# Strassen's seven products for a split-float32 w_up, with token blocks of 264, in a one-core decoder trunk

## The chip, the cores and the metric

The kernel runs on one core of one Trainium2 chip. The metric is device time in microseconds (us) of one execution. A profiled execution gives a page and a trace with its own span. The engines are named as the profile names them: PE (matmul), PEld (its weight loads), DVE (VectorE), ACT (ScalarE), POOL (GpSimd), SP (SyncE, whose queue issues the DMAs).

## The reference, cut to what matters

One layer runs over 1024 prompt tokens and 8 sample sequences of 4 tokens, 1056 tokens in all. The model width is 1024; the FFN is 2 x 2816 wide. Everything is float32.

```
mixed = (sigmoid(m_a) * br_a + sigmoid(m_b) * (gl_1 * sigmoid(gl_2))) @ w_out   # gl = gelu(ys) @ w_s5_glu
x  = layer_norm(DN_ALPHA * x + g1 * mixed, ln1_g, ln1_b)
u2 = x * (1 + sc2) + sh2                    # sc2, sh2 per sequence
hf = u2 @ w_ffn_up                          # 1024 -> 2 x 2816
f  = (silu(hf[..., :2816]) * hf[..., 2816:]) @ w_ffn_down
x  = layer_norm(DN_ALPHA * x + g2 * f, ln2_g, ln2_b)
```

What comes before (w_in, an RG-LRU branch, an S5 state-space branch, w_lru_out) is the same in both kernels.

## The kernel before, in words

**Products.** Features lie on the 128 partitions, tokens along the free axis. A float32 number x is kept as hi (x rounded to float32r, which PE multiplies at the faster rate) and lo (x - hi, again float32r). A product is hi·hi + hi·lo + lo·hi: three matmuls for each k tile of 128 features, all summed in one PSUM bank (`mm`, L328). The tokens go in three blocks of 352 (`NB`), so one output tile of 128 features by 1056 tokens over 8 k tiles is 3 x 8 x 3 = 72 matmuls of 352 columns.

**Weights.** `WTile` holds one weight tile. Its load (L207, on SP's queue) brings the raw float32 tile; `split` makes the hi part by an ACT copy (L216) and the lo part by a subtraction (`lo_part`, which ends in the helper `tt`, L108), in two halves, of 512 columns when the tile has 8 k tiles. The subtraction runs on POOL (`self.e = P`), and on DVE for some tiles of w_out and of the last w_down part. The list `seq` fixes the order of the tiles; loads run up to three ahead of use, and the next tile is split while the current one is multiplied.

**Helpers.** All DVE and POOL tensor-tensor operations stand at L108 (`tt`), the scalar-tensor-tensor ones at L117 (`stt`). In the changed kernel the same helpers stand at L113 and L122.

**Order of work.** `tick()` stands ahead of each token block of a product; `later(n, fn)` hands a piece of work to the n-th tick from now. Beyond that each engine runs its instructions in the order in which the program writes them.

**Stages.** GLU: 16 tiles of w_glu, each by the three token blocks; the gate arithmetic is done by DVE, and the mixed activations are split by ACT and POOL into region `r2` (from L1129). w_out: all eight tiles stay in SBUF and the blocks of tokens go through them one after another (`by_tokens`). The residual x goes into M by DVE (L117, `m_t<-ps,small_t,m_t`). `Norm` centers M by the mean of its first tile (`center`, POOL), squares it (ACT L1217), sums it over the tiles (`add`, `add2`, DVE), and sums over the partitions with a small float32 matmul (L1228; the shift is L1205); `inv` takes the reciprocal (L1244). `norm1` subtracts the mean, multiplies by the inverse root, scales (ACT) and splits (ACT L1284, POOL) for the FFN.

**FFN.** The 22 k tiles of the hidden width go in four chunks (5, 5, 6, 6): for each hidden tile j two w_up tiles, gate and value, 72 matmuls each; then eight w_down tiles over the chunk's k tiles. Per token block the gate's evacuation is a tanh by ACT (L1344) and one DVE `stt`; the value's evacuation is a DVE product (L108, `norm_t<-norm_t,ps`), an ACT copy for hi (L1352) and a POOL subtraction for lo (`f_t<-norm_t,f_t`). The FFN's hidden activations of a chunk stay in SBUF (region `f`) until its w_down products. The last w_down part goes by blocks of tokens again, with the second norm (`norm2`) and the stores of y between.

## Time and profile before

| what | us |
| --- | --- |
| time, median of 3 runs | 1875.53 (1873.6 to 1875.69) |
| span of the profiled execution | 1876.2 |
| PE busy | 1766.6 (94%) |
| DVE busy | 974.8 (52%) |
| POOL busy | 798.3 (43%) |
| ACT busy | 619.9 (33%) |

For the profiled execution no time beside its span is given. The busy shares are averages over stages; the windows by stage and the chain of waits tell which engine sets the end. A matmul's record ends with the pipeline, so its duration in the rows (326 ns in the mean) is longer than the distance from one start to the next; that distance is what counts in a row of matmuls. The page writes the PE matmuls of a product under the line of `mm`, L328.

In the tables below "before" rows are instruction groups of the old kernel and "after" rows those of the new one; x3 means three in a row.

### The profile page before, as it was taken

The page shows a single profiled execution, that of the slowest core. Times are in us where ns is not written, and L with a number is a line of the kernel's source. Part 1 is how long each engine was busy: PE and PEld are TensorE (multiplying, and loading weights), DVE is VectorE, ACT ScalarE, POOL GpSimd, SP SyncE. Part 2 cuts the span into 40 slices and gives each one's busy share as a digit, 9 for nine tenths or more (in the row PEclk, how much of TensorE's full clock was granted, in tenths as well). Part 3 has the DMA queues.
Part 4 walks back from the last instruction along what each step waited for, and adds up shares of the span by engine and source line. Part 5 has one row for each costly group of instructions (what it writes and reads, how often), then busy time and mean ns, then how long its engine had stood idle before and what let it go on. Part 6 is the DMA issues. An engine that isn't in the chain of part 4 may idle for free.

```text
span 1876.2 us, 28961 instructions
## 1 busy us (share of the span) xinstructions
PE 1766.6 (94%) x11640; PEld 1724.6 (92%) x11640; DVE 974.8 (52%) x1560; ACT 619.9 (33%) x1212; POOL 798.3 (43%) x663
## 2 busy tenths in 40 slices
PE   6899989899898899999999799999999999999994
PEld 5899988899788899999999799999999999999984
DVE  6989999648888743333248841231132112211297
ACT  4433333345554633212224552112211221122233
POOL 3557666427666622233342543223323332233435
PEclk9999999999899899999999999999999999999997
DMA  9334544431111158533351010111111111111111
GB/s 342 108 106 135 161 146 140 130 123 60 48 41 59 48 139 246 172 123 126 137 198 65 23 45 26 43 58 49 35 51 57 46 37 43 57 46 43 51 35 67
DMA packets 89846, 171.92 MB, mean 92 GB/s; under 512 B 18928, under 2 KB 54000, under 8 KB 89712
## 3 DMA queue, kind: packets, MB, share of 16 engines
q1 hardware_dynamic: 89712, 170.07, 28.1%
q8 instruction: 91, 1.49, 0.3%
q14 instruction: 43, 0.35, 0.1%
HBM read 136.86 MB, written 29.02 MB: 88 GB/s over the span
## 4 chain that ended last, share of the span: by engine, by line
PE 60%; DVE 19%; POOL 8%; issue 8%; ACT 3%; DMA 2%; SPq 0%; POOLq 0%; ACTq 0%; DVEq 0%
PE ps L328 57%; DVE s_t L108 8%; DVE norm_t L108 2%; POOL weights_t L108 2%; POOL lru_t L108 2%; DVE m_t L108 2%; POOL r_t L108 2%; DVE left_t L108 2%; DVE s_t L760 1%; DVE m_t L117 1%; PE ps L387 1%; DVE s_t L117 1%; POOL m_t L108 1%; DVE small_r_t L472 1%; DVE small_l_t L472 0%
## 5 line engine op out<-in xcount | busy, mean ns | idle before, releaser
L328 PE MATMUL ps<-r_t,weights_t 128*128 128x352 f32 x7632 | 1262.3, 326 | 2.2 <-ACT weights_t L216 1.1
L328 PEld LDWEIGHTS ps<-r_t,weights_t 128*128 128x128 f32 x7632 | 1236.7, 191 | 15.5 <-issue 8.9
L108 POOL TENSOR_TENSOR weights_t<-small_t,weights_t 128x512 fp32r<-128x512 f32 (+2 forms) x260 | 344.0, 1341 | 598.3 <-ACT weights_t L216 542.0
L216 ACT ACTIVATE weights_t<-small_t 128x512 fp32r<-128x512 f32 (+2 forms) x262 | 145.7, 599 | 257.1 <-PE ps L328 137.1
L328 PE MATMUL ps<-f_t,weights_t 128*128 128x352 f32 x1206 | 194.5, 322 | 0.0
L328 PEld LDWEIGHTS ps<-f_t,weights_t 128*128 128x128 f32 x1206 | 193.7, 188 | 0.0
L117 DVE SCALAR_TENSOR_TENSOR norm_t<-norm_t,ps 128x352 f32<-128x352 f32 x66 | 34.4, 521 | 222.4 <-ACT norm_t L1344 222.4
L108 DVE TENSOR_TENSOR s_t<-s_t 128x128 f32<-128x128 f32 (+3 forms) x200 | 134.4, 719 | 12.7 <-ACT s_t L737 7.0
L108 DVE TENSOR_TENSOR norm_t<-norm_t,ps 128x352 f32<-128x352 f32 x66 | 34.4, 521 | 195.8 <-PE ps L328 195.6
L117 DVE SCALAR_TENSOR_TENSOR m_t<-ps,small_t,m_t 128x352 f32<-128x352 f32 (+1 forms) x120 | 68.4, 570 | 126.9 <-PE ps L328 126.8
L108 POOL TENSOR_TENSOR f_t<-norm_t,f_t 128x352 fp32r<-128x352 f32 x66 | 62.7, 951 | 154.0 <-ACT f_t L1352 154.0
L117 DVE SCALAR_TENSOR_TENSOR glu_t<-glu_t,ps 128x352 f32<-128x352 f32 x48 | 24.2, 518 | 185.3 <-PE ps L328 126.3
L328 PE MATMUL ps<-r_t,f_t 128*128 128x352 f32 x648 | 107.1, 326 | 0.1
L328 PEld LDWEIGHTS ps<-r_t,f_t 128*128 128x128 f32 x648 | 105.0, 190 | 1.6 <-issue 0.5
L1352 ACT ACTIVATE f_t<-norm_t 128x352 fp32r<-128x352 f32 x66 | 32.8, 498 | 200.9 <-DVE norm_t L108 200.9
L117 DVE SCALAR_TENSOR_TENSOR lru_t<-lru_t 128x1056 f32<-128x1056 f32 (+1 forms) x52 | 81.9, 1574 | 30.6 <-ACT lru_t L998 16.6
L108 POOL TENSOR_TENSOR m_t<-m_t,norm_t 128x352 f32<-128x352 f32 x58 | 62.4, 1101 | 76.7 <-ACT norm_t L1206 64.8
L117 DVE SCALAR_TENSOR_TENSOR lru_t<-lru_t,small_t 128x352 f32<-128x352 f32 (+2 forms) x96 | 87.9, 916 | 3.4
L1344 ACT ACTIVATE norm_t<-ps 128x352 f32<-128x352 f32 x66 | 30.6, 464 | 177.1 <-PE ps L328 177.1
L108 POOL TENSOR_TENSOR left_t<-s_t 128x512 f32<-128x512 f32 (+1 forms) x40 | 77.0, 1947 | 5.8 <-DVE s_t L108 3.5
L328 PE MATMUL ps<-f_t,r_t 128*128 128x352 f32 x378 | 63.7, 327 | 0.9 <-POOL r_t L108 0.5
L328 PEld LDWEIGHTS ps<-f_t,r_t 128*128 128x128 f32 x378 | 61.0, 188 | 2.7 <-POOL r_t L108 0.8
(210 smaller groups left out, 1586.4 us busy)
## 6 DMA issues: line engine op xcount, KB each, us to landing
small_t<-in_w_up_dram SPq DMA_DIRECT2D x44, 512.0 KB
small_t<-in_w_in_dram SPq DMA_DIRECT2D x40, 512.0 KB
small_t<-in_w_ada_dram SPq DMA_DIRECT2D x32, 512.0 KB
ada_w_t<-in_w_ada_dram SPq DMA_DIRECT2D x16, 512.0 KB
small_t<-in_w_glu_dram SPq DMA_DIRECT2D x16, 512.0 KB
small_t<-in_w_down_dram SPq DMA_DIRECT2D x16, 384.0 KB
small_t<-in_w_down_dram SPq DMA_DIRECT2D x16, 320.0 KB
d_u<-left_t SPq DMA_DIRECT2D x64, 72.0 KB
```

Source lines behind the costliest of these rows:

```text
L108: e.tensor_tensor(out, a, b, op=op)
L117: e.scalar_tensor_tensor(out, a, s, b, op0=op0, op1=op1)
L216: A.activation(self.hi[:, s], self.raw[:, s], AF.Copy)
L328: PE.matmul(out[:, :NB], a[:, k, :], x[:, h, nb, k, :], start=bool(first and n == 0 and q == 0), stop=bool(last and n == len(kts) - 1 and ...
L387: PE.matmul(b[32 * j:32 * j + 32, :128], silu_c[:, 2 * i + k, :], w.raw[:, k, 128 * j:128 * j + 128], start=i == k == 0, stop=i == 3 and k ...
L472: getattr(V, name)(*a, **k)
L760: V.tensor_tensor_scan(wf[:, 512 * r:512 * r + 512], tv[:, :512], vv[:, r].rearrange("p n c -> p (n c)"), 0.0, op0=OP.mult, op1=OP.add)
L1344: A.activation(p, b[:, :NB], AF.Tanh, scale=0.5)
L1352: A.activation(frr[:, 0, nb, k, :], p, AF.Copy)
```

## The change: what it does

From the GLU on the tokens go in four blocks of 264 (`Q`), by a new `mmq`. PSUM gives six rotating banks there; two more hold the sums of a norm.

w_out runs in two passes, token blocks 0 and 2 first (p = 0), 1 and 3 then (p = 1), so its tiles are loaded and split twice. The four token blocks pair up: blocks s and s + 2 form the two token halves of "s". After each pass, `norm_jobs` makes the mean and inverse root for its pair, and `operand_steps` the seven operands that Strassen's products (in Winograd's form) need: sums and differences of the two feature halves and the two token halves, each split into hi and lo. The residual of s = 0 is stored to DRAM (`d_x`) and read back later.

w_up: for hidden tile j the 2 x 2 block matrix has gate and value as its outputs and the two halves of the 1024 features as its inputs. `prep` makes seven weight operands of 4 k tiles (512 columns) from the two raw tiles: four DVE additions, seven ACT copies (hi), seven subtractions (lo: on POOL, or on DVE for most in the first units). Seven products of 4 x 3 = 12 matmuls take the place of eight, for each j and each s. `UNITS` orders them: hidden tiles 0 to 2 for s = 0, the same for s = 1, and from tile 3 on both s together, product by product. `prep` runs three products ahead (`LEAD`), with a ring of five places. `up_evac` adds the products up and makes the gate on two token blocks at once (264 x 2 = 528 columns): the last product v = 6 of an s is followed by a DVE addition, a POOL product, an ACT copy, a POOL subtraction, and a DMA that stores the finished hidden tile to DRAM (`d_f`).

w_down reads the hidden tiles back from DRAM (`f_load`, 1.08 MB each) into the places of the operands that are done with: 14 of them during the last unit and the rest later, on the same SP queue as the w_down tiles. It goes in five parts, `DOWN`, and the last part by token blocks with the second norm.

The matmuls that change are 6480 of 352 columns (GLU 1152, w_out 576, w_up 3168, w_down 1584) into 8112 of 264 (GLU 1536, w_out 768, w_up 22 x 2 x 7 x 12 = 3696, w_down 2112). The other 3456 stay.

```diff
-CHUNKS = (5, 5, 6, 6)
+DOWN = ((0, 4), (4, 8), (8, 13), (13, 16), (16, 22))
+Q = 264
+UNITS = [(j, (0,)) for j in range(3)] + [(j, (1,)) for j in range(3)] + [(j, (0, 1)) for j in range(3, FFT)]
...
-            self.e = V if key[0] == "out" and key[1] > 1 or key[0] == "down" and key[1] in DOWN_V else P
+            self.e = P
...
+    for p in range(2):
         for m in range(8):
-            queue("down", io["w_down"][m][:, k0:k0 + kc], (k0, m), nk=kc)
-        k0 += kc
-
-    # w_out, and w_down's last part, stay whole: they go through the blocks of tokens
+            queue("out", io["w_out"][m], (p, m))
+    for k0, k1 in DOWN:
+        for m in range(8):
+            queue("down", io["w_down"][m][:, k0:k1], (k0, m), nk=k1 - k0)
...
+    def mmq(out, w, x, kts, first=True, last=True, check=False):
+        kts = list(kts)
+        for n, k in enumerate(kts):
+            for q, (a, h) in enumerate(((w.hi, 0), (w.hi, 1), (w.lo, 0))):
+                PE.matmul(out[:, :Q], a[:, k, :], x(h, k), start=bool(first and n == 0 and q == 0),
+                          stop=bool(last and n == len(kts) - 1 and q == 2), skip_group_check=check)
+    def glu_product(w, evac):
+        for q in range(4):
+            tick()
+            b = bank()
+            mmq(b, w, lambda h, k: r1w[:, h, k, Q * q:Q * q + Q], range(8))
+            evac(q, b)
...
+    banks[0] = 6
...
+    def normal(ln, s, c):
+        for q in (s, s + 2):
+            x = halves(M[:, q])[:, :, 2 * c:2 * c + 2]
+            for h in range(2):
+                tt(V, x[:, h], x[:, h], over(ln.b[q][0][:, None, :Q], 2, Q), OP.subtract)
+            for h in range(2):
+                tt(V, x[:, h], x[:, h], over(ln.r[q][:, None, :], 2, Q), OP.mult)
...
+    def to_operand(e, v, s, c, x):
+        o, f = operand(v, s), operand(v, s, FT)
+        A.activation(o[:, 0, 2 * c:2 * c + 2], x, AF.Copy)
+        lo_part(e, o[:, 1, 2 * c:2 * c + 2], x, f[:, 0, 2 * c:2 * c + 2])
...
+        b11, b12, b21, b22 = t
+        return (
+            lambda: (modulated(s, 0, c, b11), modulated(s + 2, 0, c, b12)),
+            lambda: (to_operand(P, 1, s, c, b11), modulated(s + 2, 1, c, b22)),
+            lambda: (tt(V, b11, b12, b11, OP.subtract), to_operand(V, 2, s, c, b11)),
+            lambda: (tt(V, b12, b22, b12, OP.subtract), to_operand(P, 3, s, c, b12)),
+            lambda: (tt(V, b11, b22, b11, OP.subtract), to_operand(V, 0, s, c, b11), modulated(s, 1, c, b21)),
+            lambda: (to_operand(P, 5, s, c, b22), to_operand(V, 4, s, c, b21)),
+            lambda: (tt(V, b21, b21, b11, OP.subtract), to_operand(P, 6, s, c, b21)),
...
+    ring = [(wb, 1024 - z), (wb, 3072 - z), (xa, 56 * Q), (wb, z), (wb, z + 2048)]
...
+    LEAD = 3
...
+        g, p = raw4[2 * u % 4], raw4[(2 * u + 1) % 4]
+        a11, a12, a21, a22 = g[:, :4], g[:, 4:], p[:, :4], p[:, 4:]
+        if v == 0:
+            tt(V, s1t, a21, a22, OP.add)
+            tt(V, s2t, s1t, a11, OP.subtract)
+        if v == 3:
+            tt(V, a21, a11, a21, OP.subtract)
+        if v == 5:
+            tt(V, s2t, a12, s2t, OP.subtract)
+        src = (s2t, a11, s1t, a21, a12, s2t, a22)[v]
+        rg, o = ring[i % 5]
+        w = parts[i] = Part()
+        w.hi, w.lo = rg.v(o, 4, 128, t=FR), rg.v(o + 512, 4, 128, t=FR)
+        A.activation(w.hi, src, AF.Copy)
+        lo_part(V if len(UNITS[u][1]) == 1 and v % 3 != 2 else P, w.lo, src, rg.v(o, 4, 128))
+        if v == 6:
+            later(1, unit_load, u + 2)
...
+    for p in range(2):
+        for m in range(8):
+            w = use_w("out", (p, m))
+            for q in (p, p + 2):
                 tick()
+                mmq(b, w, lambda h, k: mixr[:, q, h, k, :], range(8))
+                block(ln, q, m, b, 16)
...
+        a, b, c = (bk[i][:, :Q] if i in bk else None for i in "abc")
+        cc, u2, ff = ev[bk["set"]]
+        c21, c22, f1, f2 = cc[:, 0], cc[:, 1], ff[:, 0], ff[:, 1]
+        if v == 1:
+            A.activation(c21, a, AF.Copy)
+            tt(V, u2, b, c21, OP.add)
+        elif v == 3:
+            tt(V, c22, b, c21, OP.add)
+            tt(V, c22, c, c22, OP.add)
+        elif v == 4:
+            A.activation(f1, a, AF.Tanh, scale=0.5)
+            stt(V, f1, f1, 1.0, a, OP.add, OP.mult)
+        elif v == 5:
+            tt(V, u2, c, u2, OP.add)
+            A.activation(f2, u2, AF.Tanh, scale=0.5)
+            stt(V, f2, f2, 1.0, u2, OP.add, OP.mult)
+        elif v == 6:
+            tt(V, c21, b, c21, OP.add)
+            tt(P, ff, ff, cc, OP.mult)
+            A.activation(fb[:, 0, :, s], ff, AF.Copy)
+            lo_part(P, fb[:, 1, :, s], ff, fbf[:, 0, :, s])
+            SP.dma_start(d_f[j].rearrange("p h (a s t) -> p h a s t", a=2, s=2)[:, :, :, s], fbf[:, :, :, s])
...
+    order = [(i, v) for v in range(7) for i in range(2)]
+    slots = order[:8] + order[8:13] + [order[13], (1, 7), order[0]] + order[1:7]
...
+    def f_load(k):
+        SP.dma_start(f_tile(k, FT), d_f[k])
...
+    for u, (j, ss) in enumerate(UNITS):
+        bk = {s: {"set": s if len(ss) > 1 else u % 2} for s in ss}
+        for v in range(7):
+            for s in ss:
+                tick()
+                k = "bacbacb"[v]
+                if v < 3:
+                    bk[s][k] = bank()
+                w, x = parts[7 * u + v], operand(v, s)
+                mmq(bk[s][k], w, lambda h, k: x[:, h, k, :], range(4), first=v < 3, check=True)
+                up_evac(j, v, s, bk[s])
+                if u == n - 1:
+                    f_load(slots.index((s, v)))
+            prep(7 * u + v + LEAD)
+            if u == n - 1 and v == 0:
+                residual_in(2)
+                cap[0] = first_down + 1
+                pump()
+            if u == n - 1 and v == 3:
+                cap[0] = len(seq)
+                pump()
+                split_to(first_down + 1)
...
+    for c, (k0, k1) in enumerate(DOWN[:-1]):
+        for m in range(8):
+            w = use_w("down", (k0, m))
+            for q in (0, 1, 3, 2):
+                tick()
+                b = bank()
+                mmd(b, w, q, k0, k1)
+                residual(b, 40, q, m)
+        for k in ((15, 16, 17, 18), (19, 20, 21), (), ())[c]:
+            f_load(k)
...
+    ws = [next_w("down", (LASTK, m)) for m in range(8)]
+    for q in ORDQ:
+        for m in range(8):
+            tick()
+            if q == ORDQ[0]:
+                split_to(seq.index(ws[min(m + 2, 7)]) + 1)
+            b = bank()
+            mmd(b, ws[m], q, LASTK, FFT)
+            block(ln, q, m, b, 40, q == 0 and m == 7)
+        if q:
+            later(2, ln.sums, q)
+            later(2, inv2, q)
+            for k in range(8):
+                later(3 + 2 * k // 3, norm2, q, k, P if k % 3 == 0 else V)
```

Three places of the programs, engine by engine.

POOL inside the FFN before (weights_t is the lo part of a w_up tile's half, f_t<-norm_t,f_t the lo part of a hidden tile's block of tokens):

```order
L108 TENSOR_TENSOR f_t<-norm_t,f_t 128x352 x3
L108 TENSOR_TENSOR weights_t<-small_t,weights_t 128x512 x4
L108 TENSOR_TENSOR f_t<-norm_t,f_t 128x352 x3
L108 TENSOR_TENSOR weights_t<-small_t,weights_t 128x512 x2
L108 TENSOR_TENSOR weights_t<-small_t,weights_t 128x256
```

POOL across the border between two double units after (weights_t and xa_t<-… 128x512 are lo parts of weight operands; small_t<-small_t and resid_t<-resid_t,small_t 128x528 are the products of gate and value for s = 0 and s = 1, r_t their lo parts):

```order
L113 TENSOR_TENSOR weights_t<-small_t,weights_t 128x512
L113 TENSOR_TENSOR small_t<-small_t 128x528
L113 TENSOR_TENSOR r_t<-small_t,r_t 128x2x264
L113 TENSOR_TENSOR resid_t<-resid_t,small_t 128x528
L113 TENSOR_TENSOR r_t<-resid_t,r_t 128x2x264
L113 TENSOR_TENSOR xa_t<-resid_t,xa_t 128x512
```

The product of gate and value moved from DVE to POOL; at the border four POOL instructions on hidden tiles stand between the lo part of the next unit's second weight operand (first row) and that of its third (last row).

DVE in one tick of w_out's second block of tokens before, with the first norm of the block ahead beside it:

```order
L117 SCALAR_TENSOR_TENSOR m_t<-ps,small_t,m_t 128x352
L108 TENSOR_TENSOR norm_t<-norm_t,m_t 128x352
L108 TENSOR_TENSOR m_t<-m_t,norm_t 128x352
L108 TENSOR_TENSOR m_t<-m_t,small_t 128x352
L108 TENSOR_TENSOR norm_t<-m_t,small_t 128x32
L108 TENSOR_TENSOR norm_t<-norm_t,small_t 128x32
L108 TENSOR_TENSOR norm_t<-norm_t 128x352
```

DVE in the first Strassen unit after (resid_t and small_t 128x528 are the first norm of s = 1 on two tiles of 264; 128x512 with weights_t or resid_t are weight operands; r_t and xa_t are activation or weight operands; what reads ps evacuates products or takes a norm's mean):

```order
L113 TENSOR_TENSOR resid_t<-small_t,resid_t 128x512
L113 TENSOR_TENSOR resid_t<-resid_t,ps 128x528 x2
L113 TENSOR_TENSOR resid_t<-resid_t 128x528 x2
L113 TENSOR_TENSOR resid_t<-resid_t,ps 128x528 x2
L113 TENSOR_TENSOR resid_t<-resid_t 128x528 x2
L113 TENSOR_TENSOR small_t<-ps,small_t 128x264 x2
L113 TENSOR_TENSOR weights_t<-small_t,weights_t 128x512
L113 TENSOR_TENSOR resid_t<-resid_t,small_t 128x32 x4
L122 SCALAR_TENSOR_TENSOR small_t<-small_t,ps 128x264
L113 TENSOR_TENSOR resid_t<-resid_t 128x512
L113 TENSOR_TENSOR resid_t<-resid_t,small_t 128x512
L113 TENSOR_TENSOR xa_t<-resid_t,xa_t 128x512
```

The norm of s = 1, the weight operands and the operand differences now stand in one DVE row with the evacuations of the first products.

SP's queue around the last w_down part before:

```order
L207 DMA small_t<-in_w_down_dram 128x640 x8
L207 DMA small_t<-in_w_up_dram 128x1024 x12
L207 DMA small_t<-in_w_down_dram 128x768 x8
L207 DMA small_t<-in_w_up_dram 128x1024 x12
L207 DMA small_t<-in_w_down_dram 128x768 x8
```

SP's queue during the last Strassen unit after (xa_t and r_t<-d_f are the hidden tiles that come back):

```order
L1499 DMA xa_t<-d_f 128x2112
L1499 DMA r_t<-d_f 128x2112
L1485 DMA resid_t<-d_x 128x2112
L216 DMA small_t<-in_w_down_dram 128x512
L1499 DMA xa_t<-d_f 128x2112
L1499 DMA r_t<-d_f 128x2112
L1499 DMA xa_t<-d_f 128x2112
L1499 DMA r_t<-d_f 128x2112
L1499 DMA xa_t<-d_f 128x2112
L1499 DMA r_t<-d_f 128x2112
L216 DMA small_t<-in_w_down_dram 128x512 x3
```

The loads of hidden tiles stand ahead of the second, third and fourth w_down tile in the queue.

## The prediction

> **What bounds the kernel now.** I read the page's busy shares first, then windows by stage (w_out with the first norm from 950, the norm's middle from 1041, the FFN from 1082, its last part from 1770), then the chain of waits.

> ```profile
> PE 1766.6 (94%) x11640; PEld 1724.6 (92%) x11640; DVE 974.8 (52%) x1560; ACT 619.9 (33%) x1212; POOL 798.3 (43%) x663
> core 0: us, PE busy (x) PEld busy (x) DVE busy (x) ACT busy (x) POOL busy (x), PEclk, DMA share, GB/s
> 950.00:1082.00 132.00, 120.40 (x757) 116.48 (x756) 103.75 (x180) 61.86 (x118) 60.10 (x55) 0.97 0.25 89
> 1041.00:1080.00 39.00, 30.85 (x194) 30.46 (x192) 33.59 (x42) 23.51 (x47) 25.80 (x23) 0.93 0.08 28
> 1082.00:1770.00 688.00, 688.00 (x4278) 687.75 (x4277) 144.79 (x273) 147.22 (x295) 221.13 (x208) 1.00 0.14 45
> 1082.73 686.91 PE ps L328 x4272
> ```

> In the FFN PE is never idle: DVE works 21% of it, POOL 32%. There only the number of matmuls and the price of one count. The chain's one step gives that price: 686.91 / 4272 = 160.8 ns for a matmul of 352 columns. In the w_out window PE lacks 132.00 - 120.40 = 11.6 us, and DVE, at 103.75, is the engine closest behind.

> **The columns.** 6480 matmuls of 352 become 8112 of 264. No product of 264 float32r columns is in the trace; small float32 ones are, of 136 columns (two start together, 0.23 us from the next two: 115 ns each) and of 352 (the first record of a pair ends 0.292 us before the second: 0.75 - 0.458).

> ```profile
> 176.56 0.39 PE L797 MATMUL ps<-left_t,s_t 128*128 128x136 f32 x2
> 176.79 0.39 PE L798 MATMUL ps<-s_t,left_t 128*128 128x136 f32 x2
> 1040.59 0.75 PE L1205 MATMUL ps<-m_t,small_t 128*128 128x352 f32 x2
> L1205 PE MATMUL ps<-m_t,small_t 128*128 128x352 f32 x12 | 4.5, 458 | 0.0
> ```

> These two give 0.82 ns for a column and some 4 ns fixed. With half that for a float32r column the 160.8 leave 16.5 ns fixed, and 264 columns cost 125 ns. Bounds: 120.6 in proportion to columns; 142 on the straight line from 115 at 136 to 160.8 at 352. I take 125, since the float32 pair shows a price nearly proportional to columns. Before: 6480 x 0.1608 = 1042.0 us; now 8112 x 0.125 = 1014.0: **-28** (-64 to +110). By stage: GLU +7, w_out +3, w_up -47, w_down +9. So the seventh part saved on w_up is all there is to win, and the other stages pay for the shorter block.

> [...]

> **The border between double units.** Nineteen units do two s at once: 168 matmuls, 21.0 us at 125 ns, against 144 x 0.1608 = 23.2 us for the two tiles before. What can hold PE is a weight operand whose lo part POOL has not made.

> ```profile
> L108 POOL TENSOR_TENSOR weights_t<-small_t,weights_t 128x512 fp32r<-128x512 f32 x130 | 167.9, 1312 | 331.4 <-ACT weights_t L216 287.4 <-DMA small_t<-in_w_ada_dram 43.6 <-POOL r_t L108 0.2
> L108 POOL TENSOR_TENSOR f_t<-norm_t,f_t 128x352 fp32r<-128x352 f32 x66 | 62.7, 951 | 154.0 <-ACT f_t L1352 154.0
> L216 ACT ACTIVATE weights_t<-small_t 128x512 fp32r<-128x512 f32 x130 | 74.7, 622 | 132.9 <-DMA small_t<-in_w_glu_dram 45.3 <-DMA small_t<-in_w_lru_out_dram 42.9 <-PE ps L328 27.3
> L1344 ACT ACTIVATE norm_t<-ps 128x352 f32<-128x352 f32 x66 | 30.6, 464 | 177.1 <-PE ps L328 177.1
> L108 DVE TENSOR_TENSOR norm_t<-norm_t,ps 128x352 f32<-128x352 f32 x66 | 34.4, 521 | 195.8 <-PE ps L328 195.6
> ```

> Count from the end of product 5 of the second s. DVE adds (0.43, scaled from 0.521), ACT makes the tanh (0.40) and then, behind it in its own order, the hi of the next unit's second operand (0.62); POOL makes its lo (1.31): 2.76. Product 6 of the first s ended at 1.5, so POOL goes on with its gate product of 528 columns (1.35, from 951 at 352 and 1312 at 512), waits for the ACT copy (0.64), makes the lo (1.35); the same for the second s; and only then comes the lo of the third operand (1.31). Together 2.76 + 6.68 + 1.31 = 10.75, and 0.3, an estimate, for the hand-overs: 11.05. PE has six products before it needs that operand: 72 x 0.125 = 9.0. It waits 2.05 us, at 18 borders: **+37**. Below: nothing, if POOL is a quarter quicker. Above +59, if each of its eight operations here takes 0.15 longer, as the 1.47 of the row further down against 1.31. Throughput is no trouble: POOL has 7 x 1.31 + 4 x 1.35 = 14.6 us of work in 21. A double unit then lasts 23.05 us, and in the steady part Strassen saves a tenth of a us on a pair of tiles.

> **The second w_out pass and units 0 to 2.** PE has 384 + 3 x 84 matmuls here, 79.5 us. DVE has 210 instructions by its order: 93 of 512 or 528 columns, 81 of 232 or 264, 4 reciprocals, 32 of 32 columns.

> ```profile
> L108 DVE TENSOR_TENSOR weights_t<-small_t,weights_t 128x512 fp32r<-128x512 f32 x2 | 1.3, 682 | 0.0
> L108 DVE TENSOR_TENSOR s_t<-left_t 128x256 f32<-128x256 f32 x6 | 2.3, 419 | 0.0
> L1244 DVE RECIPROCAL small_t<-norm_t 128x352 f32<-128x352 f32 x6 | 14.1, 2354 | 0.2
> L108 DVE TENSOR_TENSOR norm_t<-m_t,small_t 128x32 f32<-128x32 f32 x8 | 1.5, 192 | 0.7
> ```

> 93 x 0.68 + 81 x 0.43 + 4 x 1.77 + 32 x 0.19 = 111 us. The next rows are of the window from 1041; the last two, of the timeline, show that a DVE operation beside a POOL one takes 1.27 where it takes 0.52 alone.

> ```profile
> L108 DVE TENSOR_TENSOR m_t<-m_t,norm_t 128x352 f32<-128x352 f32 x8 | 7.5, 934 | 0.0
> L108 DVE TENSOR_TENSOR norm_t<-norm_t,m_t 128x352 f32<-128x352 f32 x7 | 6.7, 952 | 1.3 <-POOL m_t L108 1.1
> L108 DVE TENSOR_TENSOR m_t<-m_t,small_t 128x352 f32<-128x352 f32 x8 | 6.5, 809 | 0.3
> L108 DVE TENSOR_TENSOR norm_t<-norm_t 128x352 f32<-128x352 f32 x7 | 5.8, 825 | 2.9 <-ACT norm_t L1217 2.9
> L108 DVE TENSOR_TENSOR norm_t<-norm_t,small_t 128x352 f32<-128x352 f32 x1 | 1.2, 1230 | 0.1
> L108 POOL TENSOR_TENSOR weights_t<-small_t,weights_t 128x512 fp32r<-128x512 f32 x4 | 5.8, 1469 | 0.3 <-POOL r_t L108 0.2
> 1060.59 1.27 DVE L108 TENSOR_TENSOR m_t<-m_t,norm_t 128x352 f32<-128x352 f32 x1
> 1061.90 0.52 DVE L108 TENSOR_TENSOR m_t<-m_t,small_t 128x352 f32<-128x352 f32 x1
> ```

> 31 operations take 27.7 us, and would take 31 x 0.521 = 16.2 alone: 11.5 us for the window's 23 POOL operations, 0.50 us each. The stretch has 61 (41 in the pass, 20 in the units): 31 us. DVE needs 142 us, PE waits 142 - 79.5 = 62.5, of which 11.6 was waited before: **+51**. Bounds: +20 without collisions; +66 at 0.75 for each POOL operation, +82 with the waits for ACT and POOL that the window shows (4.5 in 39 us, so 16 in 142). The first pass (DVE about 22 us beside 48 of PE) and units 3 to 5 (33 beside 31.5) I put at nothing; PE covers them, and without that cover they cost the 2 us.

> **Hidden tiles through DRAM.** Each stored tile is 1.08 MB; the page's first slice shows what the queues move when nothing else counts, 342 GB/s.

> ```profile
> GB/s 342 108 106 135 161 146 140 130 123 60 48 41 59 48 139 246 172 123 126 137 198 65 23 45 26 43 58 49 35 51 57 46 37 43 57 46 43 51 35 67
> ```

> That is 3.16 us a tile. On SP's queue nine such transfers stand ahead of the second w_down tile: 28 us, begun 1.5 us into the last unit of 23 and issued only as its products end, so that tile lands some 10 us after the unit. It is due 6 us after (48 matmuls), with its split some 5 us late; six more tiles stand ahead of the fifth, which may be late by as much. The stores of the units before, 1.08 MB in 23 us, lie beside products. **+10** (0 to +25).

> **The last w_down part.**

> ```profile
> 1769.47 3.04 PE L328 MATMUL ps<-f_t,weights_t 128*128 128x352 f32 x18
> 1830.32 17.71 PE L328 MATMUL ps<-f_t,r_t 128*128 128x352 f32 x108
> L108 POOL TENSOR_TENSOR weights_t<-small_t,weights_t 128x384 fp32r<-128x384 f32 x34 | 34.4, 1015 | 63.0 <-ACT weights_t L216 55.1 <-PE ps L328 8.0
> ```

> Before, it took 1848.03 - 1769.47 = 78.6 us for 432 matmuls, 69.5 of work: 9.1 waited. Now a block of 264 is 18 us of PE. DVE has 22 operations in its sums and residual (9.5), the inverse (3.5) and five of eight tiles of the norm (4.3), and 13 POOL collisions (6.5): 23.8, three times 5.8 too much; in the first block POOL has 8 lo parts in two pieces (16 x 1.015) and 7 centers (7 x 0.75): 21.5, 3.5 too much. 17.4 + 3.5 - 9.1 = **+12** (-5 without collisions, +20 if the split falls late too). After the last matmul 1876.2 - 1848.0 = 28.2 us are left, more than half of it vector work on 352 columns, now 264: **-4**.

> Sum: 1876.2 - 28 + 37 + 51 + 10 + 12 - 4 = **1954**. The profiled execution stands 0.7 us above the median of the runs, 1875.53, and I leave that out.

> **Rivals.**
> *POOL is quick enough.* [...] If an operation of 528 columns took 1.0 us (the chain then is 11.05 - 6 x 0.34 = 9.0: from there the border costs nothing) and DVE lost nothing beside it, the sum is -28 + 0 + 20 + 10 - 5 - 4 = -7: **1869**, 1859 with the transfers hidden. For it speaks that POOL is idle two thirds of the FFN; against it, that 1312 is a mean of 130 operations beside a nearly idle DVE. 0.19.
> *Everything collides.* Stretch +82, border +59, transfers +25, last part +20, less 32: **2030**. For it: the 1.23 and 1.27 us of the DVE rows quoted above. Against: POOL has pauses. A matmul of 135 ns instead of 125 would lead there too (+81, less what it covers). 0.19.
> *Columns cost less.* At 120.6 ns only the 3708 matmuls outside the stretch, the double units and the last part gain, since in those three PE waits for other engines: 16 us, **1938**, inside the main range; 0.07. [...]
> That the change does not do what it says I rule out: the order has 3696 matmuls for w_up, not 4224.

> **How the numbers follow.** Main case 0.55, its own range 1905 to 1995. Faster than 0.2% (about what a measurement of this kernel tells from no change) is nearly all of the POOL rival and a little of the main case: 0.20; within 0.2% 0.03; slower 0.77. For eight in ten I leave out half of the two outer cases: 1855 to 2015.

> **What would show it.** Right: between 264-column matmuls 125 ns; PE idle about 2 us once per double unit, before the third operand, released by POOL's lo part; DVE busy without pause through the second pass and units 0 to 2 with PE waiting for it some 60 us; the second w_down tile's split waiting for its DMA. Wrong: a double unit of 21 us, DVE rows of 264 at 0.43 beside POOL, or matmuls far from 125.

## The result and the profile after

The changed kernel takes 2039.78 us (median of 4 runs, 2036.31 to 2044.6) against 1875.61 (1873.6 to 1875.87): a ratio of 1.0876, interval 1.0856 to 1.0896. That is 164 us slower, where 78 were forecast, and above the forecast's upper end of 2015. The profiled execution has a span of 2040.8 us.

The head of the page of the changed kernel:

```profile
span 2040.8 us, 33649 instructions
PE 1795.1 (88%) x13284; PEld 1734.6 (85%) x13284; DVE 1174.3 (58%) x2018; ACT 708.6 (35%) x1441; POOL 986.3 (48%) x816
```

PE is busy 28.5 us longer than before although the columns are cheaper, and now idle for 12% of the span. The windows by stage tell where. First the kernel before (GLU, w_out with the first norm, the FFN up to its last part, the last part, the end); the columns are the stretch, its length, then busy time and instructions of PE, PEld, DVE, ACT, POOL, the granted clock and the DMA.

```profile
768.00:964.00 196.00, 196.00 (x1417) 189.44 (x1415) 58.30 (x78) 40.44 (x82) 64.64 (x55) 1.00 0.35 128
964.00:1064.00 100.00, 96.56 (x600) 94.41 (x593) 84.16 (x157) 47.57 (x92) 41.91 (x40) 1.00 0.28 97
1064.00:1770.00 706.00, 697.84 (x4330) 696.55 (x4329) 158.63 (x291) 158.90 (x316) 234.61 (x219) 0.99 0.14 45
1770.00:1848.00 78.00, 74.37 (x444) 71.21 (x442) 65.70 (x107) 29.82 (x58) 35.97 (x35) 1.00 0.13 41
1848.00:1876.00 28.00, 4.56 (x9) 2.47 (x8) 19.67 (x28) 9.95 (x18) 13.16 (x13) 0.65 0.24 84
```

Then the changed kernel: GLU, first pass of w_out, second pass, units 0 to 2, units 3 to 5, the nineteen double units, the first four w_down parts, the last part, the end.

```profile
768.00:968.00 200.00, 200.00 (x1803) 194.61 (x1802) 47.64 (x103) 42.85 (x98) 66.27 (x63) 1.00 0.36 126
968.00:1015.00 47.00, 47.00 (x387) 46.87 (x387) 32.00 (x62) 16.85 (x37) 32.87 (x33) 1.00 0.53 182
1015.00:1102.00 87.00, 61.61 (x408) 57.80 (x408) 66.71 (x109) 37.45 (x76) 44.42 (x39) 0.84 0.26 86
1102.00:1180.00 78.00, 45.86 (x254) 41.91 (x252) 59.19 (x98) 33.97 (x66) 23.77 (x17) 0.76 0.17 55
1180.00:1232.00 52.00, 39.63 (x251) 36.76 (x252) 28.59 (x49) 16.92 (x34) 17.68 (x12) 0.87 0.27 92
1232.00:1724.00 492.00, 430.99 (x3198) 419.38 (x3197) 190.22 (x343) 149.31 (x311) 278.10 (x210) 0.93 0.27 93
1724.00:1925.00 201.00, 190.13 (x1533) 189.19 (x1533) 71.88 (x191) 34.18 (x80) 57.01 (x74) 0.97 0.42 152
1925.00:2017.00 92.00, 80.47 (x600) 77.59 (x598) 75.86 (x135) 35.28 (x78) 51.69 (x59) 0.94 0.13 41
2017.00:2041.00 24.00, 4.16 (x11) 2.58 (x9) 15.52 (x30) 8.52 (x18) 6.86 (x8) 0.57 0.24 76
```

GLU lost 4 us, w_out 34 (134 against 100), the FFN up to its last part 117 (823 against 706), the last part 14; the end won 4. Together 165, the difference of the spans.

What a matmul of 264 columns costs, the chain of waits shows in w_down, where PE is not held:

```profile
1760.66 155.23 PE ps L1543 x1263
```

155.23 / 1263 = 122.9 ns; in the best stretch below it is 121. So all 8112 cost 982 us at 121, and the columns alone won 60. 225 us were lost beside them, to PE's waits and to matmuls that come slower: the granted clock, 0.99 in the FFN before, is 0.93 over the double units and 0.76 over units 0 to 2.

A border between two double units, on PE's timeline (start, length, the instructions merged; in brackets the idle time before and what ended it) and on POOL's:

```profile
1405.79 1.62 PE L1156 MATMUL ps<-r_t,weights_t 128*128 128x264 f32 x12
...
1410.91 1.69 PE L1156 MATMUL ps<-xa_t,weights_t 128*128 128x264 f32 x12 [0.61 <-DVE small_t L113]
...
1417.96 0.51 PE L1156 MATMUL ps<-xa_t,weights_t 128*128 128x264 f32 x2 [1.00 <-ACT weights_t L1419]
1420.07 2.57 PE L1156 MATMUL ps<-xa_t,weights_t 128*128 128x264 f32 x10 [1.60 <-POOL weights_t L113]
```

```profile
1411.79 1.77 POOL L113 TENSOR_TENSOR small_t<-small_t 128x528 f32<-128x528 f32 x1
1414.31 1.32 POOL L113 TENSOR_TENSOR r_t<-small_t,r_t 128x528 fp32r<-128x528 f32 x1 [0.75 <-ACT r_t L1477]
1415.59 1.12 POOL L113 TENSOR_TENSOR resid_t<-resid_t,small_t 128x528 f32<-128x528 f32 x1
1417.46 1.32 POOL L113 TENSOR_TENSOR r_t<-resid_t,r_t 128x528 fp32r<-128x528 f32 x1 [0.75 <-ACT r_t L1477]
1418.74 2.97 POOL L113 TENSOR_TENSOR weights_t<-resid_t,weights_t 128x512 fp32r<-128x512 f32 x2
```

The unit begins at 1410.91, after PE waited 0.61 for its bank. The third operand comes in at 1417.96: first its hi part is late by 1.00 (ACT's copy stands behind ACT's copies of hidden tiles, which wait for POOL), then, two matmuls on, its lo part by 1.60, behind POOL's four operations on hidden tiles. The ten matmuls behind the second wait take 2.57 us; twelve undisturbed ones take 1.62.

### The profile page after: what moved, and what is told of

The parts are those of the page before. It is cut to its first block, busy times and chain, and to the rows that moved or that the text cites. A ratio compares the mean times of both kernels' runs of the same rounds, so it can differ in the third digit from the quotient of the medians.

```text
span 2040.8 us, 33649 instructions
## 1 busy us (share of the span) xinstructions
PE 1795.1 (88%) x13284; PEld 1734.6 (85%) x13284; DVE 1174.3 (58%) x2018; ACT 708.6 (35%) x1441; POOL 986.3 (48%) x816
## 5 line engine op out<-in xcount | busy, mean ns | idle before, releaser
L113 POOL TENSOR_TENSOR weights_t<-small_t,weights_t 128x512 fp32r<-128x512 f32 (+3 forms) x266 | 339.7, 1291 | 497.5 <-ACT weights_t L225 425.1
L328 PE MATMUL ps<-r_t,weights_t 128*128 128x352 f32 x3384 | 571.8, 329 | 1.5 <-ACT weights_t L225 1.1
L328 PEld LDWEIGHTS ps<-r_t,weights_t 128*128 128x128 f32 x3384 | 554.3, 193 | 11.4 <-issue 7.7
L1156 PE MATMUL ps<-r_t,weights_t 128*128 128x264 f32 x3780 | 510.9, 293 | 28.4 <-ACT weights_t L225 14.5
L1156 PEld LDWEIGHTS ps<-r_t,weights_t 128*128 128x128 f32 x3780 | 491.2, 196 | 36.6 <-ACT weights_t L225 15.5
L1156 PE MATMUL ps<-xa_t,weights_t 128*128 128x264 f32 x1476 | 228.1, 306 | 75.0 <-POOL weights_t L113 27.7
L1156 PEld LDWEIGHTS ps<-xa_t,weights_t 128*128 128x128 f32 x1476 | 207.4, 207 | 87.5 <-ACT weights_t L1419 37.3
L113 DVE TENSOR_TENSOR small_t<-ps,small_t 128x264 f32<-128x264 f32 (+1 forms) x268 | 100.2, 385 | 246.3 <-ACT small_t L1462 124.9
L122 DVE SCALAR_TENSOR_TENSOR resid_t<-ps,small_t,resid_t 128x264 f32<-128x264 f32 (+1 forms) x192 | 92.5, 482 | 143.0 <-PE ps L1543 130.9
L113 POOL TENSOR_TENSOR weights_t<-resid_t,weights_t 128x512 fp32r<-128x512 f32 x69 | 91.5, 1334 | 146.3 <-ACT weights_t L1419 146.3
L1543 PE MATMUL ps<-xa_t,weights_t 128*128 128x264 f32 x768 | 132.7, 288 | 12.5 <-ACT weights_t L225 10.6
L122 DVE SCALAR_TENSOR_TENSOR glu_t<-glu_t,ps 128x264 f32<-128x264 f32 (+1 forms) x56 | 25.5, 467 | 200.6 <-PE ps L1156 141.3
L1543 PE MATMUL ps<-r_t,weights_t 128*128 128x264 f32 x768 | 131.1, 286 | 0.0
L1543 PEld LDWEIGHTS ps<-xa_t,weights_t 128*128 128x128 f32 x768 | 110.4, 191 | 13.6 <-ACT weights_t L225 11.0
L1543 PEld LDWEIGHTS ps<-r_t,weights_t 128*128 128x128 f32 x768 | 109.6, 191 | 0.0
L113 POOL TENSOR_TENSOR resid_t<-resid_t,small_t 128x264 f32<-128x264 f32 (+1 forms) x86 | 76.0, 901 | 58.4 <-ACT small_t L1229 43.4
```

The costliest lines, as they stand in the source:

```text
L113: e.tensor_tensor(out, a, b, op=op)
L122: e.scalar_tensor_tensor(out, a, s, b, op0=op0, op1=op1)
L328: PE.matmul(out[:, :NB], a[:, k, :], x[:, h, nb, k, :], start=bool(first and n == 0 and q == 0), stop=bool(last and n == len(kts) - 1 and ...
L1156: PE.matmul(out[:, :Q], a[:, k, :], x(h, k), start=bool(first and n == 0 and q == 0), stop=bool(last and n == len(kts) - 1 and q == 2), sk ...
L1543: PE.matmul(b[:, :Q], a[:, n, :], f[:, h, Q * q:Q * q + Q], start=n == i == 0, stop=k == k1 - 1 and i == 2)
```

## The experiments

A time without an interval is that of one execution, and is read by stage; the kernel before took 1875 to 1876 us beside each.

**e1: the weight operand is prepared ahead of the product pair** (double units only).

```
         for v in range(7):
+            if len(ss) > 1:
+                prep(7 * u + v + LEAD)
             for s in ss:
...
-            prep(7 * u + v + LEAD)
+            if len(ss) == 1:
+                prep(7 * u + v + LEAD)
```

> Edit: in the double units the next weight operand is prepared ahead of a product pair and its evacuation, so the lo part of the third operand no longer stands behind the four POOL operations on hidden tiles. Theory A (PE waits at each border for POOL's chain, and the slow matmuls behind each wait are the clock's answer to the wait): a double unit falls from 25.9 us to about 21.5 (168 x 0.121 = 20.4 and the 0.75 us that the first product waits for its bank), 18 x 4.3 = 78 us less, about 1962. Theory B (the slow matmuls have another cause, such as the kernel's load): only the waits of 2.9 us go, 1990. If the chain is not the cause: 2040.

1946.58 us, 93 less. Ten of its double units in one window, and all nineteen:

```profile
1379.00:1582.00 203.00, 203.00 (x1679) 203.00 (x1678) 97.97 (x180) 71.33 (x150) 142.51 (x111) 1.00 0.33 106
1233.00:1623.00 390.00, 387.70 (x3190) 386.68 (x3190) 183.59 (x334) 144.90 (x305) 269.04 (x207) 1.00 0.34 112
```

PE is never idle in the ten, at 203 / 1679 = 120.9 ns a matmul, and the clock is back at 1.00. A double unit takes 20.3 us where two w_up tiles took 23.2: with the same work on every engine, only in another order, Strassen does pay in the steady part, 2.9 us for each hidden tile. Theory A held: waits and slow matmuls went together. It had allowed for a wait for the bank at each border; that went too, hence 93 us and not 78.

**e2: the product of gate and value on DVE.**

```
-            tt(P, ff, ff, cc, OP.mult)
+            tt(V, ff, ff, cc, OP.mult)
```

> Edit: the product of gate and value goes back to DVE, nothing else. Theory A: POOL's chain at the border is shorter by 2 x 1.4 = 2.8 us, about the whole wait of 2.9: a double unit of 22 us, about 1970. Rival (DVE operations beside POOL ones are stretched, so the product costs 1.3 on DVE and delays the bank's evacuation instead): 24.5 us a unit, about 2015.

1969.46 us, double units of 22.0, as theory A had it. The chain through POOL sets the border; taking a fifth of POOL's work away wins 70 of the 93 us that moving the operand ahead of it won.

**e3: eight PSUM banks beside e1's order.** Edit: `banks[0] = 8` from unit 6, 6 again before w_down.

> Edit: the one before, first run of this call, and eight rotating PSUM banks instead of six through the double units. Theory A: the first product of a unit no longer waits 0.75 us for the evacuation of product 6 from the same bank: 18 x 0.75 = 14 us less than that run, about 1948, with double units of 20.7 us. If the bank is not what it waits for: the same time as that run.

1947.58, the same as e1. In e1's double units PE waits 1.2 us in all for DVE's evacuations, against 11.4 in the changed kernel: the wait for the bank had gone with the new order, so two more banks had nothing left to win. What they would do in the old order was not run.

**e4 and e8: waits put into the kernel before.** A gate tile's lo part is made several times, so that it comes late.

```
-                lo_part(self.e, self.lo[:, s], self.raw[:, s], hf[:, s])
+                for _ in range(again):       # 8 in e4, 12 to 24 in e8, at 13 gate tiles
+                    lo_part(self.e, self.lo[:, s], self.raw[:, s], hf[:, s])
```

> Edit on the kernel before: for 13 gate tiles of w_up the second half's lo part is made eight times instead of once, so PE, which had no wait there, waits some 3 us at each for 9 us more of POOL work. Output unchanged. Theory A (a wait of this size is followed by matmuls at a lower granted clock): the time grows by more than the waits, some 13 x (3 + 2) = 65 us, 1940, with the granted clock in the up stages near 0.93. Theory B: by the waits alone, 13 x 3 = 39, 1915, with the clock at 1.00 in those stages.

1873.83: no wait arose, 9 us more of POOL work at a tile were covered. It does not tell the theories apart, but serves as a control for e8: POOL is busy 332 of the 680 us below (the kernel before has 221 in the 688 us of the FFN), PE never waits, and the granted clock stays at 1.00.

```profile
1085.00:1765.00 680.00, 680.00 (x4246) 680.00 (x4246) 141.31 (x269) 142.97 (x287) 332.07 (x295) 1.00 0.15 45
```

> Edit on the kernel before: as in e4_before_with_waits, but the lo part is made 12 to 24 times at 13 gate tiles, so that waits of graded length arise in a stretch in which PE otherwise never waits and no other engine is near its limit. Theory A (a wait by itself brings the granted clock down): from some length on, 10 to 25 matmuls behind a wait come about 1.8 times as far apart, near 290 ns instead of 160, and the granted clock of the up stages falls below 0.95; the time is the waits plus 1 to 3 us each. Theory B (it takes the load of the Strassen stretch): spacing stays at 160 ns behind every wait.

2051.02 us, with waits of 5 to 21 us. Two stretches of w_up tiles in the kernel before, and the same in e8; then one of e8's waits:

```profile
1250.00:1365.00 115.00, 115.00 (x720) 115.00 (x720) 16.39 (x32) 23.41 (x48) 37.61 (x34) 1.00 0.13 40
1423.00:1561.00 138.00, 138.00 (x864) 138.00 (x863) 19.48 (x38) 28.45 (x58) 45.72 (x41) 1.00 0.13 43
```

```profile
1249.00:1400.00 151.00, 123.53 (x719) 122.38 (x718) 16.17 (x33) 23.09 (x48) 100.59 (x84) 0.90 0.10 30
1457.00:1672.00 215.00, 150.29 (x865) 148.85 (x864) 19.67 (x38) 29.23 (x59) 153.28 (x126) 0.83 0.09 27
```

```profile
1269.76 4.00 PE L332 MATMUL ps<-r_t,weights_t 128*128 128x352 f32 x24
1278.65 6.64 PE L332 MATMUL ps<-r_t,weights_t 128*128 128x352 f32 x30 [4.89 <-POOL weights_t L108]
```

The same 720 matmuls keep PE busy 123.5 us instead of 115.0, the 864 150.3 instead of 138.0, with nothing changed but the waits (4 and 5 long ones): about 2 us for each. By the starts in the trace, 8 to 17 matmuls behind each wait stand some 290 ns apart, then 160 again; a wait of 21 us is followed by no more of them than one of 5. Theory A: the clock answers to the wait. In the last part of the kernel before, waits of 0.9 and 1.8 us leave the granted clock at 1.00.

**e5 and e6: order in the stretch of w_out's second pass and the single units.** e5 gives seven weight tiles of the second pass places in `r2` and splits them two ahead (`split_to(seq.index(w) + 3)`); e6 prepares first in the single units as well.

> Edit on e1_prep_first: in w_out's second pass seven of the eight weight tiles get places of their own in the mixed activations that the first pass has read, and are split two tiles ahead instead of one. Theory H (PE waits in that pass because ACT's copy of the next weight tile stands behind the norm's ACT work, 17 us of waits and the slow matmuls behind them): the pass falls from 86.7 us to about 62, the total by 25, 1922. Theory D (DVE is the bound of the whole stretch, as the prediction had it): the pass gets shorter but DVE's backlog moves into units 0 to 2, whose 78.9 us grow by as much; total within 8 us of 1946.6.

> Edit on e1_prep_first: the weight operand is prepared first in the single units too. Theory H (order: lo parts stand behind the evacuation's POOL chain here as well): units 3 to 5 fall from 52.6 us to about 36, units 0 to 2 by some 8, total 1922. Theory D (DVE is the bound in units 0 to 2, 59 us busy of 79): units 3 to 5 still fall, units 0 to 2 stay; total 1930. If neither: 1946.

1945.98 and 1945.12: nothing. From the second pass to unit 5, e1 takes 218 us, e5 217, e6 216. In e5 PE's waits for the copies of weight tiles shrink (13.7 us to 8.3) and the one at the norm's sums grows from 7.3 to 12.5; theory D. In e6 units 3 to 5 fall by 3 us only, not by 17: in e1 PE waits there for the parts of weight operands, in e6 10.3 of its 11.9 us for DVE's evacuations, and DVE in turn 11.1 us for ACT's copies of weight operands. My reading that the order at the border is what holds these units was wrong; the wait moved.

**e7: the hidden tiles' loads paced.** Edit: the first w_down tile is loaded one unit earlier; ten hidden tiles of the last unit, and one more, are issued one or two after each w_down tile of the first part.

> Edit on e1_prep_first: the first w_down tile is loaded in the unit before the last, four hidden tiles come back ahead of the other w_down tiles, and the other eleven are issued one or two after each w_down tile. Theory (the first w_down part waits 10.8 us for its weight tiles, because SP's queue moves 1.08 MB tiles ahead of them, and ACT's copy, waiting for the DMA, holds the last tanh): that part falls from 61.4 us to about 48, total 1933. If the waits come from elsewhere: 1946.

1936.3 us, 10 less: the last unit falls from 24.7 to 20.3 us, the first w_down part from 61.4 to 54.4 (46.5 without waits). So more than half of the price of DRAM was the place in the queue.

**g1: one hidden tile through single units instead of three**; **g2: their lo parts on POOL**; **g4: the norm's additions left out.**

```
-UNITS = [(j, (0,)) for j in range(3)] + ... + [(j, (0, 1)) for j in range(3, FFT)]
+UNITS = [(j, (0,)) for j in range(1)] + ... + [(j, (0, 1)) for j in range(1, FFT)]      # g1
...
-        lo_part(V if len(UNITS[u][1]) == 1 and v % 3 != 2 else P, w.lo, ...)
+        lo_part(P, w.lo, ...)                                                           # g2
...
-                    tt(V, a1, a1, x, OP.add)                                            # g4, first norm
-            tt(V, self.a2[q], self.a2[q], self.square(q, k), OP.add)
```

In g1 the ring of weight operands did not fit 23 units, so that the last operand of the last unit is overwritten before its product; the amount of work is the same.

> Edit on e7_loads_paced: one hidden tile instead of three goes through single units (s = 0, then s = 1), the other 21 through double units; the norm of s = 1 is emitted within the one unit of s = 0. Weight operands are then prepared 23 times instead of 25. Theory D (vector work, DVE's above all, bounds the stretch from the second w_out pass to unit 5, 218 us for 108 us of PE work): four preparations of 7 operands fewer in the stretch and two double units more at 20.3 us, total lower by about 20, 1916. Rival W (the single units are the cover that PE has while the norm of s = 1 is made): PE waits for that norm instead, total the same or up to 15 higher, 1936 to 1951.

> Edit on e7_loads_paced: in the single units all lo parts of weight operands are made by POOL, none by DVE; 30 DVE operations of about 0.8 us move. Theory D (DVE's own work is the bound): units 0 to 5 fall by some 20 of 131 us, 1916. Rival L (in-order chains between the engines, an operand's ACT copy and its lo part, are the bound; POOL takes 1.3 us where DVE takes 0.7): no gain, or a loss of up to 15, 1936 to 1951.

> Edit on e7_loads_paced: leaves out the DVE additions that sum the residual and its square over the feature tiles for the first norm (28 operations in the second w_out pass, about 19 us there by the trace, as many in the first pass), so the first norm's mean and variance are those of one tile. Theory D (DVE's work bounds the stretch): the time falls one for one, some 19 us, 1917. Rival L (the chains between the engines bound it): 5 us or less, 1931 or more.

g1: 1910.82 us, 25.5 less: theory D, though rival W is there too, since PE waits 21.9 us for DVE's evacuations in the two units that are left. g2: 1927.78, 8.5 less, where 20 or nothing was expected. g4: 1923.56, 12.7 less for 28 DVE operations in the second pass (the 28 of the first pass are missing as well, but that pass takes 47.6 us in both). The second pass in e7 and, without the additions, in g4:

```profile
1014.00:1101.00 87.00, 62.57 (x415) 59.02 (x415) 67.06 (x110) 37.27 (x75) 44.56 (x40) 0.85 0.26 86
```

```profile
1014.00:1087.00 73.00, 57.89 (x416) 55.82 (x415) 46.00 (x72) 34.74 (x71) 43.07 (x40) 0.88 0.31 102
```

DVE does 21 us less there and the pass ends 14 us earlier. So vector work bounds this stretch, but not one for one: DVE is idle for 23% of it in the one and 37% in the other, and two thirds of what is taken off it is won.

**g3: the last part's sums two ticks later.** Edit: `later(4, ln.sums, q)` and the norm behind it, instead of `later(2, ...)`.

> Edit on e7_loads_paced: in the last w_down part the sums over partitions of a block are issued four ticks into the next block instead of two, its norm two ticks later. Theory (PE waits 5.3 and 4.1 us at the sums, in order, for DVE's additions, with slow matmuls behind): the last part falls from 92 us to about 82, total 1926. Theory D' (DVE is at its limit in these blocks, 21 us busy of 25): the waits move to the end, 1934 to 1937.

1932.43, 4 less, between the two expectations. In the changed kernel PE waits at the sums (first row); in g3 at the next block's first small product instead (second row), for the same DVE:

```profile
PE ps L1250 <- DVE small_t L113: 9.5, 3, 4.4
```

```profile
PE ps L1228 <- DVE resid_t L122: 9.3, 2, 5.3
```

A moved wait, not one removed.

**h1: the edits e1, e6, e7, g1, g2, g3 together, the ring mended; h2: beside them, half of the first norm's multiplications on POOL.**

```
-    ring = [(wb, 1024 - z), (wb, 3072 - z), (xa, 56 * Q), (wb, z), (wb, z + 2048)]
+    ring = [(xa, 56 * Q), (wb, 1024 - z), (wb, 3072 - z), (wb, z), (wb, z + 2048)]      # h1
...
-                tt(V, x[:, h], x[:, h], over(ln.r[q][:, None, :], 2, Q), OP.mult)
+                tt(V if q == s else P, x[:, h], x[:, h], over(ln.r[q][:, None, :], 2, Q), OP.mult)   # h2
```

> The edits of e1, e6, e7, g1, g2 and g3 together, with the ring of weight operands begun at another place so that it fits 23 units. Theory D (the stretch from the second w_out pass to the last single unit is bound by vector work, and the edits outside it are independent): the gains add up to about 1910.8 (g1) - 3 (lo parts of two single units on POOL instead of six, a third of g2's 8.5) - 1.5 - 4 = 1902. Rival W (cover): with two single units left, moving lo parts to POOL lengthens its chain and PE waits for that, 1908 to 1915. By either it stays above the kernel before.

> Edit on h1_all_edits: in the first norm the multiplication by the inverse root goes to POOL for one token block of each pair: 8 DVE operations of 528 columns (0.7 to 0.9 us each, 4 of each pass's norm) become POOL operations of about 1.35. Theory D (DVE's work is the bound while POOL is idle half of the stretch): some 5 us less. Rival L (collisions of DVE with POOL and the hand-overs between them cost what is taken off DVE): no gain, or up to 8 us more.

h1 takes 1905.99 us (1904.13 to 1908.05), a ratio of 1.016 to the kernel before, interval 1.0143 to 1.0177: the gains add up to within 4 us of the 1902 expected, 134 of the 164 us are won back, and it is still slower than before. In its two single units PE waits 25.5 us for DVE's evacuations. h2 takes 1908.36: no gain. The stretch from the second pass to the last single unit, h1 and h2:

```profile
1014.00:1168.00 154.00, 94.45 (x577) 87.90 (x576) 115.33 (x182) 67.44 (x133) 78.70 (x64) 0.78 0.20 66
```

```profile
1014.00:1168.00 154.00, 91.80 (x568) 85.34 (x567) 113.48 (x173) 65.30 (x128) 88.90 (x70) 0.76 0.20 63
```

POOL does 10 us more and DVE only 2 less, though eight operations of some 0.8 us left it: DVE's other operations grew, the 24 like them that stayed from 0.83 to 0.99 us each. That is rival L. Less vector work helps; moving it from DVE to POOL does not.

## Why the prediction was wrong

**Direction, and what bounds.** Slower was right (0.77), and so were the places: the border, the second pass with units 0 to 2, the loads, the last part. The size was half of the measured one, and the two largest terms were too small.

**Columns, -28: measured -60.** 125 ns came from half of a float32 column, an assumption that no run shows (at 352 columns the trace before has 160.8 ns for float32r and 0.29 us for float32, a pair of L1205), and the fixed 16.5 ns that it left; measured are 121, in proportion to the 160.8 of 352 columns: the lower bound. The float32 pair already showed a price nearly without a fixed part, and I should have taken it.

**Border, +37: measured +106** (492 us for 3192 matmuls of 121 ns, 386). This is the step that failed. The chain was right in kind, and e1 and e2 show it, but 2.05 us were forecast for a border and 5.9 were lost at one: the chain was too short, and a price for the granted clock was missing. First, the lo part was not the only wait: the same queue of work also held the operand's hi part on ACT and, through DVE, the first product's bank. The waits by releaser in the double units:

```profile
PE ps L1156 <- POOL weights_t L113: 24.1, 16, 1.6
PE ps L1156 <- ACT weights_t L1419: 15.2, 15, 1.0
PE ps L1156 <- DVE small_t L113: 11.4, 18, 1.0
PE ps L1156 <- POOL xa_t L113: 5.6, 4, 1.6
PE ps L1156 <- ACT xa_t L1419: 3.0, 3, 1.0
```

59 us in all, of the 61 that PE lacks in that window. From start to start they cost 70 us, 3.9 at a border, because the record of the matmul before a wait runs some 0.16 us past the usual distance (in w_down a record is some 284 ns long, the distance 122.9) and counts as busy. Second, the chain took longer. At the border shown above it runs from the end of product 5 (1405.79 + 1.62 = 1407.41) to 1420.07: 12.66 us, where 11.05 were forecast. Nearly all of the difference lies ahead of POOL's first gate product (1411.79): 4.38 us for the 2.76 of the sum. There DVE's half of the gate of the first s runs beside a POOL operation and holds the addition of the second s back; it takes 1.21 us in the mean, the same operation of the second s 0.48:

```profile
L122 DVE SCALAR_TENSOR_TENSOR small_t<-small_t 128x264 f32<-128x264 f32 x19 | 23.0, 1213 | 13.5 <-ACT small_t L1472 13.5
L122 DVE SCALAR_TENSOR_TENSOR resid_t<-resid_t,small_t 128x264 f32<-128x264 f32 x20 | 9.5, 477 | 10.0 <-ACT resid_t L1472 10.0
```

From there to the third operand's lo part it took 6.95 us for 6.68. Third, and not in any term of the sum: the remaining 35 us are 345 matmuls that follow one another at mostly 220 ns and not at 121, 1.9 us at a border, in stretches where the granted clock is 0.5. I counted a wait at its length; here it cost half as much again. The upper bound of +59 took eight POOL operations where the chain has six; with six it is +53. My sentence that throughput is no trouble was right: at e1's order POOL's 142.5 us of 203 hold nobody.

**Second pass and units 0 to 2, +51: measured +76** (87 + 78 us for 77 of PE work; of the other 88, 58 are idle and 30 slow matmuls and the ends of records, and 11.6 were there before). The term assumed that DVE would be the only limit and run without pause for 142 us. It has 125.9 us of work there, so the collisions were priced too high (15 us for 56 POOL operations, not 31), and it is idle for 39 us, some 33 of them waiting for ACT and POOL, which the sum priced at nothing (only the upper bound had 16). g4, where two thirds of the work left out was won, and h2, where work moved to POOL won nothing, fit both halves. How these 39 us divide between hand-overs and order stays open: e5 and e6 changed the order and won nothing.

**Units 3 to 5, 0: measured +21** (52 us for 31). I called DVE's 33 us a cover of 31.5; DVE has 28.6 there, and PE waits for lo and hi parts of operands. e6 won 3 of it and moved the waits to DVE's evacuations, behind ACT's copies; which order would remove them is not settled.

**Loads +10: measured +15. Last part +12: measured +14. End -4: measured -4.** The mechanisms were as described; e7 shows the queue, g3 that DVE sets the last blocks. One thing was missed in the loads: ACT's copy of the first w_down tile waits 9.62 us for its DMA with the last unit's tanh behind it.

**Rivals.** What w_up could win was an eighth of its columns, not the seventh part of the prediction's text; its -47 us are right. The column rival came true in its price, but a faster PE only waits longer at a border. The POOL rival fell: POOL's operations took 1.1 to 1.8 us. "Everything collides" gave 2030, 10 us off, but by terms that cancel: its border (+59) was too small, its stretch, loads and last part about right, its columns too dear.

## What to carry to other kernels

Work for the next unit that is issued behind the evacuation of the current one waited for that evacuation: POOL ran its operations in the order written, and at the border shown above the lo part of the third operand began 6.95 us after the first of the four operations on hidden tiles. Issue the operand first, which here was one moved line and 93 us. A wait of PE cost more than its length where the granted clock fell behind it: about 2 us more in e8, 1.9 at a border of the changed kernel (next section). A saving in matmuls is worth only what the operands' vector work, counted with its hand-overs, leaves: here an eighth fewer products won 2.9 us for each hidden tile, and making the operands took it back in the stretch that has no cover.

## What the runs showed of the hardware

```profile
1259.12:1262.53 3.41, 2.40 (x20) 2.19 (x19) 0.00 (x0) 1.45 (x3) 2.66 (x3) 1.00 0.40 139
1262.53:1265.95 3.42, 1.82 (x14) 1.61 (x14) 1.82 (x3) 2.27 (x6) 3.42 (x3) 1.00 0.50 178
1416.13:1419.55 3.42, 1.33 (x9) 0.91 (x8) 0.82 (x3) 2.76 (x6) 2.67 (x3) 1.00 0.46 158
1419.55:1422.96 3.41, 2.89 (x13) 2.90 (x14) 1.01 (x1) 1.15 (x2) 3.41 (x4) 0.50 0.45 161
```

The clock falls sixteen times in the double units, each time behind a window in which PE was idle for 51 to 61%; the windows there with PE idle for up to 47% were not followed by a fall. (Between the second w_out pass and the double units two windows of 51 and 52% were not, so near a half the trace shows both.) In the kernel before, a wait of 3.31 us lies across two windows and the clock stays:

```profile
1030.40:1033.81 3.41, 1.81 (x12) 1.52 (x10) 3.20 (x8) 1.84 (x4) 0.93 (x1) 1.00 0.00 0
1033.81:1037.22 3.41, 1.71 (x7) 1.31 (x8) 3.20 (x7) 1.46 (x4) 0.93 (x1) 1.00 0.02 5
```

In the double units alone the slow matmuls cost 35 us, 1.7% of the changed kernel's span of 2040.8 us.

In e7 a DVE operation that reads one operand from PSUM was not slowed beside POOL, one that reads both from SBUF was. From 700 us on, the evacuations `small_t<-ps,small_t` of 264 columns took 432 ns where they ran mostly beside POOL (154 of them) and 428 alone (56). In e7's second pass, the norm's subtraction (mean in PSUM) and its multiplication and the operands' differences (all in SBUF), of the same 528 columns:

```profile
L113 DVE TENSOR_TENSOR resid_t<-resid_t,ps 128x528 f32<-128x528 f32 x8 | 5.2, 694 | 0.0
L113 DVE TENSOR_TENSOR resid_t<-resid_t 128x528 f32<-128x528 f32 x16 | 13.8, 887 | 2.5 <-POOL xa_t L113 2.5
```

Of the sixteen in the second row, eleven ran alone and took 699 ns in the mean; five had POOL at work for most of their time and took 1301.
